# A second form of h2 for the later tiles of an up projection: normalised on the spot, with new homes for f, gates and split tiles

## The chip, the cores and the metric

The kernel runs on one core of one Trainium2 chip, as one program with one launch. The metric is the device time of an execution in microseconds (us). TensorE (PE) multiplies, VectorE (DVE) and ScalarE (ACT) do the elementwise work, GpSimd (POOL) and SyncE (SP) mostly start transfers. Each engine works through its own queue of instructions in order, and waits at an instruction until what it needs is there.

## The reference

One layer of a hybrid backbone over 384 tokens: 128 context tokens and 256 latent tokens, with 2048 channels. Context and latent tokens have modulation vectors of their own (scale, shift and gate, from a conditioning vector). First comes a mixer with three branches and an output projection, then the gated feed-forward part that matters here:

```python
x = x + g1 * rmsnorm(mix, norm_mix_post)
h2 = rmsnorm(x, norm_ffn_pre) * (1 + sc2) + sh2
u, g = jnp.split(h2 @ w_ffn_up, 2, axis=-1)
g = along_cols(lambda t: dwconv(t, ffn_conv_w, ffn_conv_b), g, rows)
f = (jax.nn.gelu(g) * u) @ w_ffn_down
x = x + g2 * rmsnorm(f, norm_ffn_post)
```

`w_ffn_up` is 2048 x 11264, `w_ffn_down` 5632 x 2048, all in float32. The root mean square in `rmsnorm` is over the channels, so its factor is one number per token.

## The kernel before

Activations lie with channels on the 128 partitions and the 384 tokens along the free axis, in 16 tiles of channels, the k tiles. To keep float32 accuracy, both operands of a product are split into a high part (rounded to the matmul's format) and a low part (the rest), and three matmuls are accumulated: high x high, high x low, low x high. Such a group of three is called a triple. ACT writes the high part (L169), DVE the low part (L170).

All weights come through one stream, a list of pieces in the order of use. `run_stream` walks along it. For each piece it issues, in this order: the splits of the pieces up to two ahead (three buffers each for high and low parts, so a split waits until PE has left the piece three before it); if the piece has a `before` function, first the pending `after` functions of the piece ahead of it and then `before`; the matmuls; the pending `after` functions if they are still to be run; and then one step from each of three queues of background work, `bgq[0..2]`, a second one from `bgq[2]` if more than two are left there.

The up projection has 88 tiles of 128 output channels, in turn u and g of the same channels, so that tiles 2n and 2n+1 form pair n. Tiles 0 to 5 are computed together, k tile by k tile (`up0_use`, pieces of 768 columns), while h2 is being made (`h2_step`). Tiles 6 to 87 follow one at a time, each in two pieces of 8 k tiles; piece (t, p) is part p of tile t below. Each tile takes one of four accumulator banks in rotation, and each pair is worked off by three steps on `bgq[2]`: `first` (read the banks), `taps` (the convolution), `last` (Gelu and product), called the after-steps.

The kernel does not wait for the token factor r3 = 1/rms(x) before tile 0. It multiplies the weights with x * S2, where S2 is (1 + sc2) times the norm's weight, and corrects afterwards. The shift is handled by four further columns of the moving operand: H2 for context and latent tokens, as high and low parts (`full`, 388 columns). `first` multiplies the products with r3, and adds the two halves of the shift's products (`hb`), which `taps` and `last` then add as biases. r3 is computed in `close_mx`, which is in the `after` list of the last combined piece: `token_sums` on PE, a Sqrt on ACT, a reciprocal on DVE, a broadcast by PE into a bank, and ACT's copy from there.

Beside the up projection run: the gate g2 (`ada2`, 32 pieces of weights multiplied on DVE with the conditions `MX["cb"]`, which are broadcast by POOL's DMAs and put through a Sigmoid), the transposes of x (`turn_x2`, from tile 12), and `finish_g2`. After it the down projection reads f, 44 k tiles in two halves of the output channels.

Buffers have homes by tag: `hx0` to `hx15` hold the split operand of the projections (448-element pitch, high and low), and pool `F["p"]`, opened in `close_mx`, holds f.

Of the kernel before, what the change touches and what calls it, by code (L numbers as in the profile page):

```python
# [94 lines left out]
def body(ctx: ExitStack, tc: tile.TileContext, i, o):  # L95
# [987 lines left out]
        zt(T_POOL + g, [pool_after(g)])  # L1083


    MX = {}
    mix = [None] * KD
    mx_cm = []

    def open_mx():  # L1090
        flush_bg()
        close_pool(zp_cm[0])
        cm, pool = open_pool("mx", "right")
        mx_cm.append(cm)
        MX["p"] = pool
        conditions(lambda n: pool.tile([P, PIECE], F32, name=name("cb"), tag=f"cb{n}"))

    def conditions(alloc):

        MX["junk"], MX["silu"] = alloc(4), 0  # L1100
        MX["cb"] = [[alloc(2 * c + h) for h in range(2)] for c in range(2)]
        def part(c, h):
            t = MX["cb"][c][h]

            def f():
                act.activation(MX["junk"], t, AF.Sigmoid)
                dve.tensor_mul(t, t, MX["junk"])
                MX["silu"] += 1

            gp.dma_start(t, i["cond2"][c : c + 1, PIECE * h : PIECE * (h + 1)].broadcast_to([P, PIECE]))  # L1110
            bgq[1].append(f)

        for c in range(2):
            for h in range(2):
                part(c, h)

    def gate_after(n, b):
# [50 lines left out]

    def ada2(m, n, half):
        def f(raw):  # L1170
            assert MX["silu"] == 4
            for c in range(2):
                dve.scalar_tensor_tensor(MX["junk"], raw, 1.0, MX["cb"][c][half], ALU.mult, ALU.mult,  # L1173
                                         accum_out=MODR[:, m, n, c, half : half + 1])

        return f
# [175 lines left out]
    fx = [None] * NF  # L1352
    NUP0 = 6

    def up_mm(ps, wh, wl, x, first, last):

        pe.matmul(ps[:, :HW], wh, x.full, start=first, stop=False, skip_group_check=True)  # L1357
        pe.matmul(ps[:, :NT], wh, x.lo, start=False, stop=False, skip_group_check=True)  # L1358
        pe.matmul(ps[:, : NT + 2], wl, x.full[:, : NT + 2], start=False, stop=last, skip_group_check=True)  # L1359
# [10 lines left out]
        return f  # L1370

    def f_tile(n):
        if n % 3 == 0:
            F["t"] = F["p"].tile([P, min(3, NF - n), NT], F32, name=name("f"), tag=f"f{n // 3}")
        return F["t"][:, n % 3]

    def up_after(n):
        st = {}

        def f():  # L1380
            bgq[2].extend((first, taps, last))

        def first():
            pu, pg = acc[("up", 2 * n)], acc[("up", 2 * n + 1)]
            r = R["r3"]
            hb = tmp("hb", 4, bufs=2)
            hb4 = tmp("hb4", 8, bufs=2).rearrange("p (a c) -> p a c", a=2)
            act.activation(hb4[:, 0], pu[:, NT:HW], AF.Copy)
            act.activation(hb4[:, 1], pg[:, NT:HW], AF.Copy)
            dve.tensor_add(hb.rearrange("p (a c) -> p a c", a=2), hb4[:, :, 0:2], hb4[:, :, 2:4])  # L1390
            g = tmp()
            dve.tensor_mul(g, pg[:, :NT], r)
            u = tmp()
            dve.tensor_mul(u, pu[:, :NT], r)
            st.update(hb=hb, g=g, u=u)

        def taps():
            g, hb = st["g"], st["hb"]
            act.activation(g[:, :SEQ], g[:, :SEQ], AF.Identity, bias=hb[:, 2:3])
            act.activation(g[:, SEQ:], g[:, SEQ:], AF.Identity, bias=hb[:, 3:4])  # L1400
            y = tmp()
            w = [v("ffn_conv_w", 3 * n + j) for j in range(3)]
            act.activation(y, g, AF.Identity, bias=v("ffn_conv_b", n), scale=w[1])
            st["y"] = y
            for dst, src, wj in (
                ((1, SEQ), (0, SEQ - 1), w[0]),
                ((0, SEQ - 1), (1, SEQ), w[2]),
                ((SEQ + GRID_W, NT), (SEQ, NT - GRID_W), w[0]),
                ((SEQ, NT - GRID_W), (SEQ + GRID_W, NT), w[2]),
            ):  # L1410
                a = y[:, dst[0] : dst[1]]
                dve.scalar_tensor_tensor(a, g[:, src[0] : src[1]], wj, a, ALU.mult, ALU.add)

        def last():
            y, u, hb = st["y"], st["u"], st["hb"]
            act.activation(y, y, AF.Gelu_apprx_tanh)
            t = f_tile(n)
            dve.scalar_tensor_tensor(t[:, :SEQ], u[:, :SEQ], hb[:, 0:1], y[:, :SEQ], ALU.add, ALU.mult)
            dve.scalar_tensor_tensor(t[:, SEQ:], u[:, SEQ:], hb[:, 1:2], y[:, SEQ:], ALU.add, ALU.mult)
            fx[n] = t  # L1420

        return f
# [5 lines left out]
    def up_use(t, part):  # L1428
        def f(hi, lo):
            if part == 0:  # L1430
                acc["up", t] = accbank()
            for a in range(8):
                k = 8 * part + a
                up_mm(acc["up", t], hi[:, a], lo[:, a], hx[k], k == 0, k == KD - 1)

        return f

    for k in range(KD):
        stream.append(Piece(i["w_up0"][k], (NUP0 * P,), up0_use(k), before=open_f if k == 0 else None,
                            after=[close_mx] + [up_after(n) for n in range(NUP0 // 2)] if k == KD - 1 else None))  # L1440
    a3 = deque()
    for n in range(KD):
        for half in range(2):
            a3.append(Piece(i["w_ada2"][3, n, :, PIECE * half : PIECE * (half + 1)], (PIECE,), None,
                            vec=ada2(3, n, half)))
    for t in range(NUP0, 2 * NF):
        for part in range(2):
            bf = None
            if t == NUP0 + 2 and part == 0:
                bf = lambda: conditions(  # L1450
                    lambda n: F["p"].tile([P, 3 * NT], F32, name=name("cb"), tag=f"f{9 + n}")[:, :PIECE])
            elif t == 2 * NF - 1 and part == 1:
                bf = lambda: down_start()
            elif t == NUP0 + 6 and part == 0:
                bf = lambda: turn_x2()
            elif t == NUP0 + 50 and part == 0:
                bf = lambda: finish_g2()
            stream.append(Piece(i["w_up"][t - NUP0, :, 8 * part : 8 * part + 8], (8, P), up_use(t, part), before=bf,
                                after=[up_after(t // 2)] if t % 2 and part else None))
        if t > NUP0 + 8 and a3:  # L1460
            stream.append(a3.popleft())
    assert not a3

# [27 lines left out]
    def g2_rows():  # L1491

        ps = bgbank()
        pe.transpose(ps[0 : 2 * KD, 0:P], G2.rearrange("p c k -> p (c k)"), ident)
        row = tmp("g2r", P, bufs=1)
        act.activation(row[0 : 2 * KD], ps[0 : 2 * KD, 0:P], AF.Copy)
        gp.dma_start(G2D.rearrange("c (k p) -> (c k) p", p=P), row[0 : 2 * KD])
        g2_load(0)

    def g2_load(h):  # L1500
        t = F["p"].tile([P, 2, HALF_D], F32, name=name("gb"), tag="gb")
        for c in range(2):
            gp.dma_start(t[:, c], G2D[c : c + 1, HALF_D * h : HALF_D * (h + 1)].broadcast_to([P, HALF_D]))
        DN["g", h] = t

    def down_start():
        down_split(0)
# [2 lines left out]
    def down_split(s):  # L1510
        if s >= 2 * NF:
            return
        pr = h_pair(f"hx{s % 3}", NT)
        split(pr.hi, pr.lo, fx[s % NF])
        DN["f", s] = pr

# [7 lines left out]
    def down_use(h, k):  # L1524
        def f(hi, lo):
            if k == 0:
                acc4 = [(rot["acc"] + c) % 4 for c in range(1, 5)]
                free = [4, 5, 6, 7] + acc4[:2] if h == 0 else acc4[2:] + [4, 5, 6, 7]
                DN["ps", h] = [bank(b) for b in free]
            ps = DN["ps", h]  # L1530
            x = DN.pop(("f", h * NF + k))
            down_split(h * NF + k + 2)
            if h == 1 and k >= NF - 3:
                DN["last"] = DN.get("last", []) + [(k, hi, lo, x)]
                if k == NF - 1:
                    down_last(ps)
                return
            for t in range(3):
                for b in range(2):
                    down_mm(ps[2 * t + b], x, hi, lo, t, b, k == 0, k == NF - 1)  # L1540
                if k == NF - 1:
                    for b in range(2):
                        down_out(h, t, b, ps[2 * t + b])
            if k == NF - 1:
                g2_load(1)
                sqrt_table()
# [3 lines left out]
    def down_out(h, t, b, ps):  # L1550

        n = 2 * h + b
        junk = hp.tile([P, NB], F32, name=name("junk"), tag="hx15")
        act.activation(junk, ps, AF.Square, accum_out=ss4[:, t, n : n + 1])
        g = hp.tile([P, NB], F32, name=name("fo"), tag=f"hx{3 + 4 * t + n}")
        dve.tensor_mul(g, ps, DN["g", h][:, min(t, 1), b * NB : (b + 1) * NB])
        fo[t, n] = g

    def down_last(ps):
# [156 lines left out]
```

## Time and profile before

| | |
|---|---|
| median of 3 runs | 2275.97 us (2275.54 to 2276.22) |
| the profiled execution's own time | 2277.23 us |
| its span, first to last instruction | 2275.4 us |
| PE busy | 2237.1 us, 98% |
| DVE busy | 1434.6 us, 63% |
| ACT busy | 881.6 us, 39% |
| mean granted PE clock | 0.993 |

In a row of the timeline stand the start in us from the span's start, the length, the engine, the line, the operation, out<-in, the shapes and the count, and in brackets how long the engine was idle before and what released it. Instructions of one engine overlap at their ends, so the next can start before the one ahead has ended. A row of the stretches view gives, for each engine, busy us and (instructions) in the order PE, weight load, DVE, ACT, POOL, and then the granted clock, the share of DMA and GB/s. A row of a line's own view gives a minimum, median and maximum in ns and the first and last start. The combined tiles 0 to 5 run until about 1208 us, tiles 6 to 87 until about 1906 us, the down projection to the end.

### The profile page before, as it was taken

What the parts mean: (1) busy time and instruction counts of PE and PEld (TensorE: products, weight loads), DVE (VectorE), ACT (ScalarE), POOL (GpSimd) and SP (SyncE); (2) the same over time, 40 slices, a digit from 0 to 9 for tenths busy, and PEclk for the clock granted to TensorE, in tenths of its full rate; (3) what the DMA queues carried; (4) which work ended last, traced back from release to release, by engine and by line L of the source; (5) the groups of instructions that cost most, each with busy time, mean ns of one, the idle gap of its engine ahead of it and who ended that gap; (6) DMA issues with size and microseconds to landing.
All of it is one profiled execution on the core that took longest, in us unless ns stands there. A gap on an engine that the chain in (4) does not pass through costs nothing.

```text
span 2275.4 us, 31790 instructions
## 1 busy us (share of the span) xinstructions
PE 2237.1 (98%) x12553; PEld 2132.7 (94%) x12553; DVE 1434.6 (63%) x2296; ACT 881.6 (39%) x1366; POOL 32.1 (1%) x73
## 2 busy tenths in 40 slices
PE   6999999999999999999989999999999999999998
PEld 3799999999999999999989999999999999888886
DVE  3466777656888888868477577775444445444445
ACT  4443333534223332243376433333333334334333
POOL 0000000000000000000000000000000000000000
PEclk8999999999999999999999999999999999999999
DMA  9944333335766676668433455554433333434343
GB/s 397 392 140 126 123 110 119 121 103 188 232 216 228 224 233 227 222 225 274 139 100 130 138 185 193 180 192 151 140 129 126 124 126 124 130 130 148 130 130 111
DMA packets 104870, 390.06 MB, mean 171 GB/s; under 512 B 12112, under 2 KB 12256, under 8 KB 100624
## 3 DMA queue, kind: packets, MB, share of 16 engines
q1 hardware_dynamic: 100080, 372.81, 48.7%
q0 software_dynamic: 4064, 14.36, 2.0%
q8 instruction: 98, 1.61, 0.3%
q10 hardware_dynamic: 576, 0.86, 0.1%
q14 instruction: 52, 0.43, 0.1%
HBM read 382.71 MB, written 5.27 MB: 171 GB/s over the span
## 4 chain that ended last, share of the span: by engine, by line
PE 96%; DVE 2%; DMA 1%; ACT 1%; issue 1%; DVEq 0%; POOL 0%; SPq 0%; ACTq 0%
PE ps L178 13%; PE ps L180 13%; PE ps L179 13%; PE ps L1357 11%; PE ps L1359 11%; PE ps L1358 11%; PE ps L1521 5%; PE ps L1522 5%; PE ps L1520 5%; PE ps L396 1%; PE ps L898 1%; PE ps L897 1%; PE ps L896 1%; DMA eraw<-w_ada 1%; PE ps L993 1%; PE ps L988 1%
## 5 line engine op out<-in xcount | busy, mean ns | idle before, releaser
L170 DVE TENSOR_TENSOR wlo<-raw,whi 128x1024 fp32r<-128x1024 f32 (+3 forms) x521 | 622.2, 1197 | 706.1 <-ACT whi L169 702.1
L169 ACT ACTIVATE whi<-raw 128x1024 fp32r<-128x1024 f32 (+3 forms) x521 | 539.9, 1039 | 1223.5 <-PE ps L1358 419.7
L178 PE MATMUL ps<-hx,whi 128*128 128x384 f32 x1616 | 546.7, 338 | 2.5 <-ACT whi L169 2.5
L180 PE MATMUL ps<-hx,wlo 128*128 128x384 f32 x1616 | 541.6, 335 | 1.4 <-DVE wlo L170 1.4
L179 PE MATMUL ps<-hx,whi 128*128 128x384 f32 x1616 | 541.4, 335 | 0.2 <-DVE hx L170 0.2
L1357 PE MATMUL ps<-hx,whi 128*128 128x388 f32 x1408 | 481.5, 342 | 4.0 <-DVE hx L1327 4.0
L1359 PE MATMUL ps<-hx,wlo 128*128 128x386 f32 x1408 | 476.6, 339 | 0.0
L1358 PE MATMUL ps<-hx,whi 128*128 128x384 f32 x1408 | 472.4, 336 | 0.0
L1173 DVE SCALAR_TENSOR_TENSOR cb<-raw,cb 128x1024 f32<-128x1024 f32 x256 | 313.2, 1224 | 8.3 <-DMA raw<-w_ada 2.2
L178 PEld LDWEIGHTS ps<-hx,whi 128*128 128x128 f32 x1616 | 304.3, 188 | 9.0 <-ACT whi L169 4.2
L180 PEld LDWEIGHTS ps<-hx,wlo 128*128 128x128 f32 x1616 | 304.2, 188 | 2.6 <-DVE wlo L170 2.6
L179 PEld LDWEIGHTS ps<-hx,whi 128*128 128x128 f32 x1616 | 304.3, 188 | 0.9 <-DVE hx L170 0.5
L1358 PEld LDWEIGHTS ps<-hx,whi 128*128 128x128 f32 x1408 | 270.9, 192 | 0.0
L1357 PEld LDWEIGHTS ps<-hx,whi 128*128 128x128 f32 x1408 | 265.0, 188 | 4.2 <-ACT hx L1313 4.2
L1359 PEld LDWEIGHTS ps<-hx,wlo 128*128 128x128 f32 x1408 | 265.3, 188 | 0.0
L1521 PE MATMUL ps<-whi,hx 128*128 128x512 f32 x528 | 205.5, 389 | 0.8 <-DVE hx L170 0.8
L1520 PE MATMUL ps<-whi,hx 128*128 128x512 f32 x528 | 205.5, 389 | 0.0
L1522 PE MATMUL ps<-wlo,hx 128*128 128x512 f32 x528 | 205.4, 389 | 0.0
L1521 PEld LDWEIGHTS ps<-whi,hx 128*128 128x128 f32 x528 | 99.1, 188 | 21.6 <-DVE hx L170 1.1
L1520 PEld LDWEIGHTS ps<-whi,hx 128*128 128x128 f32 x528 | 99.1, 188 | 21.1 <-ACT hx L169 0.4
L1522 PEld LDWEIGHTS ps<-wlo,hx 128*128 128x128 f32 x528 | 99.1, 188 | 20.4
L703 DVE SCALAR_TENSOR_TENSOR cacc<-cbuf,vec,cacc 128x444 f32<-128x444 f32 x116 | 78.8, 679 | 2.8
(298 smaller groups left out, 1742.8 us busy)
## 6 DMA issues: line engine op xcount, KB each, us to landing
raw<-w_up SPq DMA_DIRECT2D x164, 512.0 KB, 3.7
raw<-w_in SPq DMA_DIRECT2D x163, 512.0 KB, 3.9
raw<-w_ada SPq DMA_DIRECT2D x128, 512.0 KB, 4.3
raw<-w_down SPq DMA_DIRECT2D x88, 512.0 KB, 3.3
eraw<-w_ada SPq DMA_DIRECT2D x32, 1024.0 KB, 16.8
raw<-w_out SPq DMA_DIRECT2D x32, 512.0 KB, 4.6
raw<-w_v SPq DMA_DIRECT2D x16, 512.0 KB, 3.8
raw<-w_br SPq DMA_DIRECT2D x16, 512.0 KB, 4.8
```

The source lines that it names most:

```text
L169: act.activation(hi, src, AF.Copy)
L170: dve.tensor_sub(lo, src, hi.bitcast(F32))
L178: pe.matmul(out, wh, x, start=first, stop=False, skip_group_check=True)
L179: pe.matmul(out, wh, xl, start=False, stop=False, skip_group_check=True)
L180: pe.matmul(out, wl, x, start=False, stop=last, skip_group_check=True)
L1173: dve.scalar_tensor_tensor(MX["junk"], raw, 1.0, MX["cb"][c][half], ALU.mult, ALU.mult, accum_out=MODR[:, m, n, c, half : half + 1])
L1357: pe.matmul(ps[:, :HW], wh, x.full, start=first, stop=False, skip_group_check=True)
L1358: pe.matmul(ps[:, :NT], wh, x.lo, start=False, stop=False, skip_group_check=True)
L1359: pe.matmul(ps[:, : NT + 2], wl, x.full[:, : NT + 2], start=False, stop=last, skip_group_check=True)
L1520: pe.matmul(ps, xh, hi[:, w], start=first, stop=False, skip_group_check=True)
L1521: pe.matmul(ps, xl, hi[:, w], start=False, stop=False, skip_group_check=True)
L1522: pe.matmul(ps, xh, lo[:, w], start=False, stop=last, skip_group_check=True)
```

## The change

From tile 10 on the up projection uses another form of h2, `hy`: x times r3, then scale and shift, split into high and low parts of 384 columns. It is made by `h2_finals`, two k tiles at a time, in the eight pieces of tiles 6 to 9: each of these pieces gets a `before` function, which puts one call of `h2_finals` on `bgq[0]`. Tiles 10 to 87 then use the plain triple `mm3` of three 384-column matmuls. For pairs 5 and up `first` is two copies on ACT, `taps` has no bias passes, and `last` is one multiply on DVE.

`hy` takes the room of f in `F["p"]`, and f for pairs 6 to 37 moves to the `hx` tags. The split tiles of the down projection, its scratch and half of its outputs move to `hy` tags; g2's rows are loaded in four DMAs per half, the first ones from the third piece of the down projection. The conditions for g2 come in two halves (tiles 10 and 34), and its 32 pieces are ordered by half: 16 after tiles 15 to 30, 16 after tiles 38 to 53. `finish_g2` moves from tile 56 to tile 66. The DMA scratch of the program is halved. The core of the diff:

```diff
+    NH2 = 10
+    hy = [None] * KD
+    def y_pair(k, n):
+        t = F["p"].tile([P, 2, HPITCH], F32R, name=name("hy"), tag=f"hy{k}")
...
+    def h2_final(k):
+        st = {}
+        def mul():
+            st["t"] = tmp("hs2", NT, bufs=2)
+            dve.tensor_mul(st["t"], X["x"][:, k], R["r3"])
+        def mod():
+            t = st["t"]
+            act.activation(t[:, :SEQ], t[:, :SEQ], AF.Identity, bias=H2[:, k, 0:1], scale=S2[:, k, 0:1])
+            act.activation(t[:, SEQ:], t[:, SEQ:], AF.Identity, bias=H2[:, k, 1:2], scale=S2[:, k, 1:2])
+            hy[k] = y_pair(k, NT)
+            act.activation(hy[k].hi, t, AF.Copy)
+        def low():
+            dve.tensor_sub(hy[k].lo, st["t"], hy[k].hi.bitcast(F32))
+        return mul, mod, low
+    def h2_finals(k0, k1):
+        parts = [h2_final(k) for k in range(k0, k1)]
+        for n in range(len(parts) + 1):
+            if n < len(parts):
+                parts[n][0]()
+                parts[n][1]()
+            if n:
+                parts[n - 1][2]()
...
     def f_tile(n):
-        if n % 3 == 0:
-            F["t"] = F["p"].tile([P, min(3, NF - n), NT], F32, name=name("f"), tag=f"f{n // 3}")
-        return F["t"][:, n % 3]
+        if n < 6 or n >= 38:
...
+            F["t"] = hp.tile([P, 2, NT], F32, name=name("f"), tag=f"hx{(n - 6) // 2}")
+        return F["t"][:, n % 2]
...
         def first():
             pu, pg = acc[("up", 2 * n)], acc[("up", 2 * n + 1)]
+            if 2 * n >= NH2:
+                g = tmp()
+                act.activation(g, pg[:, :NT], AF.Copy)
+                u = tmp()
+                act.activation(u, pu[:, :NT], AF.Copy)
+                st.update(g=g, u=u)
+                return
...
+                if t < NH2:
+                    up_mm(acc["up", t], hi[:, a], lo[:, a], hx[k], k == 0, k == KD - 1)
+                else:
+                    mm3(acc["up", t][:, :NT], hi[:, a], lo[:, a], hy[k].hi, hy[k].lo, k == 0, k == KD - 1)
...
-            if t == NUP0 + 2 and part == 0:
-                bf = lambda: conditions(
-                    lambda n: F["p"].tile([P, 3 * NT], F32, name=name("cb"), tag=f"f{9 + n}")[:, :PIECE])
+            if t == NH2 and part == 0:
+                bf = lambda: conditions_f(0)
+            elif t == NH2 + 24 and part == 0:
+                bf = lambda: conditions_f(1)
+            elif NUP0 <= t < NH2:
+                bf = lambda q=2 * (t - NUP0) + part: bgq[0].append(lambda: h2_finals(2 * q, 2 * q + 2))
...
-        if t > NUP0 + 8 and a3:
+        if (NH2 + 4 < t and len(a3) > KD or t > NH2 + 27) and a3:
             stream.append(a3.popleft())
...
-        pr = h_pair(f"hx{s % 3}", NT)
+        pr = y_pair(s % 3, NT)
...
-    nc = bacc.Bacc("TRN2", target_bir_lowering=False, num_devices=1, dynamic_dma_scratch_size=4096)
+    nc = bacc.Bacc("TRN2", target_bir_lowering=False, num_devices=1, dynamic_dma_scratch_size=2048)
```

More of the change, by code (lines that the diff above doesn't have):

```diff
@@ L1083, in body @@
         zt(T_POOL + g, [pool_after(g)])
-    MX = {}
+    MX = {"cb": [[None, None], [None, None]]}
     mix = [None] * KD
@@ L1095, in open_mx, with conditions @@
         MX["p"] = pool
+        MX["junk"] = pool.tile([P, PIECE], F32, name=name("cb"), tag="cb4")
         conditions(lambda n: pool.tile([P, PIECE], F32, name=name("cb"), tag=f"cb{n}"))
-    def conditions(alloc):
-        MX["junk"], MX["silu"] = alloc(4), 0
-        MX["cb"] = [[alloc(2 * c + h) for h in range(2)] for c in range(2)]
+    def conditions(alloc, halves=(0, 1)):
+        MX["silu"] = {}
         def part(c, h):
-            t = MX["cb"][c][h]
+            t = alloc(2 * c + h)
+            MX["cb"][c][h] = t
             def f():
@@ L1107, in f @@
                 dve.tensor_mul(t, t, MX["junk"])
-                MX["silu"] += 1
+                MX["silu"][c, h] = True
             gp.dma_start(t, i["cond2"][c : c + 1, PIECE * h : PIECE * (h + 1)].broadcast_to([P, PIECE]))
@@ L1113, in conditions @@
         for c in range(2):
-            for h in range(2):
+            for h in halves:
                 part(c, h)
@@ L1170, in f @@
         def f(raw):
-            assert MX["silu"] == 4
             for c in range(2):
+                assert MX["silu"][c, half]
                 dve.scalar_tensor_tensor(MX["junk"], raw, 1.0, MX["cb"][c][half], ALU.mult, ALU.mult,
@@ L1353, in body @@
     NUP0 = 6
+    NH2 = 10
+    hy = [None] * KD
+    def y_pair(k, n):
+        t = F["p"].tile([P, 2, HPITCH], F32R, name=name("hy"), tag=f"hy{k}")
+        pr = Two()
+        pr.hi, pr.lo = t[:, 0, :n], t[:, 1, :n]
+        return pr
+    def h2_final(k):
[20 more added lines that the diff above has]
+                parts[n - 1][2]()
     def up_mm(ps, wh, wl, x, first, last):
@@ L1372, in f_tile @@
     def f_tile(n):
-        if n % 3 == 0:
-            F["t"] = F["p"].tile([P, min(3, NF - n), NT], F32, name=name("f"), tag=f"f{n // 3}")
-        return F["t"][:, n % 3]
+        if n < 6 or n >= 38:
+            m = n % 3 if n < 6 else (n - 38) % 3
+            if m == 0:
+                F["t"] = F["p"].tile([P, 3, NT], F32, name=name("f"), tag=f"f{n // 3 if n < 6 else 2 + (n - 38) // 3}")
+            return F["t"][:, m]
+        if n % 2 == 0:
+            F["t"] = hp.tile([P, 2, NT], F32, name=name("f"), tag=f"hx{(n - 6) // 2}")
+        return F["t"][:, n % 2]
     def up_after(n):
@@ L1397, in taps @@
         def taps():
-            g, hb = st["g"], st["hb"]
-            act.activation(g[:, :SEQ], g[:, :SEQ], AF.Identity, bias=hb[:, 2:3])
-            act.activation(g[:, SEQ:], g[:, SEQ:], AF.Identity, bias=hb[:, 3:4])
+            g = st["g"]
+            if 2 * n < NH2:
+                hb = st["hb"]
+                act.activation(g[:, :SEQ], g[:, :SEQ], AF.Identity, bias=hb[:, 2:3])
+                act.activation(g[:, SEQ:], g[:, SEQ:], AF.Identity, bias=hb[:, 3:4])
             y = tmp()
@@ L1414, in last @@
         def last():
-            y, u, hb = st["y"], st["u"], st["hb"]
+            y, u = st["y"], st["u"]
             act.activation(y, y, AF.Gelu_apprx_tanh)
             t = f_tile(n)
-            dve.scalar_tensor_tensor(t[:, :SEQ], u[:, :SEQ], hb[:, 0:1], y[:, :SEQ], ALU.add, ALU.mult)
-            dve.scalar_tensor_tensor(t[:, SEQ:], u[:, SEQ:], hb[:, 1:2], y[:, SEQ:], ALU.add, ALU.mult)
+            if 2 * n < NH2:
+                hb = st["hb"]
+                dve.scalar_tensor_tensor(t[:, :SEQ], u[:, :SEQ], hb[:, 0:1], y[:, :SEQ], ALU.add, ALU.mult)
+                dve.scalar_tensor_tensor(t[:, SEQ:], u[:, SEQ:], hb[:, 1:2], y[:, SEQ:], ALU.add, ALU.mult)
+            else:
+                dve.tensor_mul(t, u, y)
             fx[n] = t
@@ L1433, in f, with conditions_f @@
                 k = 8 * part + a
-                up_mm(acc["up", t], hi[:, a], lo[:, a], hx[k], k == 0, k == KD - 1)
-        return f
+                if t < NH2:
+                    up_mm(acc["up", t], hi[:, a], lo[:, a], hx[k], k == 0, k == KD - 1)
+                else:
+                    mm3(acc["up", t][:, :NT], hi[:, a], lo[:, a], hy[k].hi, hy[k].lo, k == 0, k == KD - 1)
+        return f
+    def conditions_f(h):
+        if h == 0:
+            MX["junk"] = F["p"].tile([P, PIECE + 8], F32, name=name("cb"), tag="junk")[:, :PIECE]
+        conditions(lambda n: F["p"].tile([P, 3 * NT], F32, name=name("cb"), tag=f"f{2 + n // 2}")[:, :PIECE], (h,))
     for k in range(KD):
@@ L1441, in body @@
     a3 = deque()
-    for n in range(KD):
-        for half in range(2):
+    for half in range(2):
+        for n in range(KD):
             a3.append(Piece(i["w_ada2"][3, n, :, PIECE * half : PIECE * (half + 1)], (PIECE,), None,
@@ L1448, in body @@
             bf = None
-            if t == NUP0 + 2 and part == 0:
-                bf = lambda: conditions(
-                    lambda n: F["p"].tile([P, 3 * NT], F32, name=name("cb"), tag=f"f{9 + n}")[:, :PIECE])
+            if t == NH2 and part == 0:
[4 more added lines that the diff above has]
+                bf = lambda q=2 * (t - NUP0) + part: bgq[0].append(lambda: h2_finals(2 * q, 2 * q + 2))
             elif t == 2 * NF - 1 and part == 1:
                 bf = lambda: down_start()
-            elif t == NUP0 + 6 and part == 0:
+            elif t == NH2 + 2 and part == 0:
                 bf = lambda: turn_x2()
-            elif t == NUP0 + 50 and part == 0:
+            elif t == NUP0 + 60 and part == 0:
                 bf = lambda: finish_g2()
@@ L1497, in g2_rows @@
         gp.dma_start(G2D.rearrange("c (k p) -> (c k) p", p=P), row[0 : 2 * KD])
-        g2_load(0)
     def g2_load(h):
-        t = F["p"].tile([P, 2, HALF_D], F32, name=name("gb"), tag="gb")
         for c in range(2):
-            gp.dma_start(t[:, c], G2D[c : c + 1, HALF_D * h : HALF_D * (h + 1)].broadcast_to([P, HALF_D]))
-        DN["g", h] = t
+            for b in range(2):
+                t = F["p"].tile([P, NB], F32, name=name("gb"), tag=f"hy{10 + 2 * c + b}")
+                gp.dma_start(t, G2D[c : c + 1, HALF_D * h + NB * b : HALF_D * h + NB * (b + 1)].broadcast_to([P, NB]))
+                DN["g", h, c, b] = t
     def down_start():
@@ L1532, in f @@
             down_split(h * NF + k + 2)
+            if h == 0 and k == 2:
+                g2_load(0)
             if h == 1 and k >= NF - 3:
@@ L1552, in down_out @@
         n = 2 * h + b
-        junk = hp.tile([P, NB], F32, name=name("junk"), tag="hx15")
+        junk = F["p"].tile([P, NB], F32, name=name("junk"), tag="hy3")
         act.activation(junk, ps, AF.Square, accum_out=ss4[:, t, n : n + 1])
-        g = hp.tile([P, NB], F32, name=name("fo"), tag=f"hx{3 + 4 * t + n}")
-        dve.tensor_mul(g, ps, DN["g", h][:, min(t, 1), b * NB : (b + 1) * NB])
+        pool, tag = (F["p"], f"hy{4 + 2 * t + b}") if h == 0 else (hp, f"hx{2 * t + b}")
+        g = pool.tile([P, NB], F32, name=name("fo"), tag=tag)
+        dve.tensor_mul(g, ps, DN["g", h, min(t, 1), b])
         fo[t, n] = g
```

## The prediction

> **What bounds the kernel now.** I read the page first (busy shares, the chain that ended last), then the PE waits from tile 6 of the up projection to the end, then the timelines of PE, ACT and DVE around tile 6, where the change begins.
>
> ```profile
> PE 2237.1 (98%) x12553; PEld 2132.7 (94%) x12553; DVE 1434.6 (63%) x2296; ACT 881.6 (39%) x1366; POOL 32.1 (1%) x73
> PE 96%; DVE 2%; DMA 1%; ACT 1%; issue 1%; DVEq 0%; POOL 0%; SPq 0%; ACTq 0%
> ```
> ```profile
> PE ps L1521 <- DVE hx L170: 0.8, 1, 0.8
> ```
> PE is the bound and the chain is PE's. The second fence is the whole answer of the PE waits from 1216 us to the end (total, times, longest): one wait of 0.8 us, at the start of the down projection. So from tile 6 on time can be won only by PE doing less, and lost as soon as DVE or ACT fall behind.
>
> **What the change takes off PE.** From tile 10 on the matmul triple is 384+384+384 columns in place of 388+384+386. The nearest rows are the triples of today's up tiles and the 384-wide triples of the merge gates, on the same kind of operand pair.
>
> ```profile
> 1854.16 0.34 PE L1357 MATMUL ps<-hx,whi 128*128 128x388 f32 x1
> 1865.75 0.34 PE L1357 MATMUL ps<-hx,whi 128*128 128x388 f32 x1
> ```
> ```profile
> 900.14 0.33 PE L178 MATMUL ps<-hx,whi 128*128 128x384 f32 x1
> 925.10 0.33 PE L178 MATMUL ps<-hx,whi 128*128 128x384 f32 x1
> ```
> Between the first two starts lie 22 triples: 11.59/22 = 0.5268 us. Between the other two lie 48: 24.96/48 = 0.5200 us. Tiles 10 to 87 have 78 x 16 = 1248 triples, so PE does 1248 x 0.0068 = 8.5 us less. The Trainium skill (TensorE: Matmul & The Clock Gate, section Back-to-back issue gap) gives a warm gap of N/2.4 + 2.5 ns; by it six columns are 2.5 ns, and the gain an estimated 3.1 us. The trace shows 6.8 ns for the six, so I take the trace.
>
> **What it costs at the start of tile 6.** Before `before()` of a piece is called, the stream runs the pending `after` work. Today piece (6,0) has no `before`, so `close_mx` (the token scale r3) is issued behind its 24 matmuls. Now it has one, and `close_mx` goes ahead of them. Also, r3 then sits in the bank that tile 6 takes next, so PE must wait for ACT's copy of r3. Around this place the trace of before has (all rows):
>
> ```profile
> 1207.96 1.06 ACT L169 ACTIVATE whi<-raw 128x1024 fp32r<-128x1024 f32 x1 [2.10 <-PE ps L1358]
> 1209.05 1.23 DVE L170 TENSOR_TENSOR wlo<-raw,whi 128x1024 fp32r<-128x1024 f32 x1 [1.93 <-ACT whi L169]
> 1212.15 0.73 PE L310 MATMUL ps<-ones,ss 128*128 128x1 f32 x6
> 1212.91 0.26 ACT L316 ACTIVATE rc<-ps,eps 128x3 f32<-128x3 f32 x1 [3.89 <-PE ps L310]
> 1213.21 0.17 DVE L317 RECIPROCAL rc<-rc 128x3 f32<-128x3 f32 x1 [2.93 <-ACT rc L316]
> 1213.44 0.93 PE L319 MATMUL ps<-ident,rc 128*128 128x128 f32 x6 [0.56 <-DVE rc L317]
> 1214.13 0.42 PE L1357 MATMUL ps<-hx,whi 128*128 128x388 f32 x1
> 1214.41 0.49 ACT L322 ACTIVATE r<-ps 128x384 f32<-128x384 f32 x1 [1.23 <-PE ps L319]
> 1214.85 0.18 ACT L1389 ACTIVATE hb<-ps 128x4 f32<-128x4 f32 x1
> 1215.06 0.17 DVE L1390 TENSOR_TENSOR hb<-hb 128x4 f32<-128x4 f32 x1 [1.68 <-ACT hb L1389]
> 1215.14 0.55 DVE L1392 TENSOR_TENSOR t<-ps,r 128x384 f32<-128x384 f32 x1
> 1215.61 0.55 DVE L1394 TENSOR_TENSOR t<-ps,r 128x384 f32<-128x384 f32 x1
> 1215.73 0.40 ACT L1399 ACTIVATE t<-t,hb 128x128 f32<-128x128 f32 x1 [0.70 <-DVE t L1392]
> 1216.04 0.49 ACT L1400 ACTIVATE t<-t,hb 128x256 f32<-128x256 f32 x1
> 1216.56 0.71 ACT L1403 ACTIVATE t<-t,vec 128x384 f32<-128x384 f32 x1
> 1217.18 1.04 ACT L169 ACTIVATE whi<-raw 128x1024 fp32r<-128x1024 f32 x1
> 1217.30 1.52 DVE L1412 SCALAR_TENSOR_TENSOR t<-t,vec,t 128x127 f32<-128x127 f32 x4 [1.15 <-ACT t L1403]
> 1218.74 1.22 DVE L170 TENSOR_TENSOR wlo<-raw,whi 128x1024 fp32r<-128x1024 f32 x1
> 1218.90 1.28 ACT L1416 ACT_TABLE_LOAD   x1 [0.68 <-DVE t L1412]
> 1220.20 0.53 ACT L1416 ACTIVATE t<-t 128x384 f32<-128x384 f32 x1
> 1220.75 0.35 DVE L1418 SCALAR_TENSOR_TENSOR f<-t,hb,t 128x128 f32<-128x128 f32 x1 [0.80 <-ACT t L1416]
> 1221.42 0.15 DVE L1390 TENSOR_TENSOR hb<-hb 128x4 f32<-128x4 f32 x1
> ```
> Today the block takes PE from 1212.15 to 1214.13, 1.98 us. The split of piece (7,0) starts at 1207.96, the moment PE leaves the last combined piece (it needs that piece's weight buffer); call it time 0. Moved ahead, the sums end at 0.73; the Sqrt and the reciprocal stand behind that split on ACT and DVE. L170 starts at 1.09; DVE issues its next instruction some 0.08 before one ends (L1392 is 0.55 long, L1394 starts 0.47 behind it), so after 1.14. The reciprocal then starts at 2.2, the broadcast at 2.45 (0.23 behind it, as above), the copy at 3.4, and with its 0.49 r3 and PE's tile 6 are free at 3.9 us. Against 1.98 that is 1.9 us more.
>
> **What it costs beside tiles 6 to 9.** The eight pieces of these tiles last 8 x 0.5268 = 4.21 us each. Each gets two k tiles of the new h2: per k tile a multiply and a subtract on DVE, and three passes on ACT. No row shows these, but the same shapes stand above and here:
>
> ```profile
> 1171.70 0.53 ACT L1313 ACTIVATE hx<-sig 128x386 fp32r<-128x386 f32 x1
> 1172.13 0.51 ACT L1320 ACTIVATE t<-x 128x384 f32<-128x384 f32 x1
> 1172.86 0.55 DVE L1326 TENSOR_TENSOR hx<-sig,hx 128x384 fp32r<-128x384 f32 x1
> ```
> DVE alone would need 2 x 0.94 us for the pair (issue 0.47, as L1392 to L1394). But both queues are in order and the work alternates: multiply 0.55; ACT 0.31 + 0.52 (as L1399, L1400, L1403 start), then the copy 0.53, issuing 0.43; the second k tile's passes follow on ACT; its subtract can only start after them. With 0.04 per handover: 0.59 + (0.31+0.52+0.43) + (0.31+0.52+0.53) + 0.04 = 3.25, plus the subtract's 0.47: DVE is held 3.7 us per pair, nearly 1.9 of it waiting. Behind the waiting subtract on DVE stand the after-steps below and then the weight split of the piece two ahead, and PE waits for that split.
>
> Behind each pair come the up projection's own after-steps of pairs 0 to 3, which the stream pops two at a time while more than two are queued. From the rows above: first 1.0 on DVE (0.08 + 2 x 0.47); taps 1.44 on DVE after 1.54 on ACT, of which some 0.6 runs under the last subtract, so 2.4; last 0.7, or 1.4 where it follows taps at once and must wait for the Gelu; the first one 1.3 more for the table. In the order popped: (6,0) first+taps 3.7; (6,1) last+first 2.95; (7,0) taps+last 3.8; (7,1) first 1.3 (0.3 waiting for a split on ACT); (8,0) taps+last 3.8; (8,1) first 1.3; (9,0) taps 2.4; (9,1) last 0.7. Sum 19.95.
>
> DVE's queue up to the split that piece (11,0) waits for: r3 3.9, eight pairs 8 x 3.7 = 29.6, after-steps 19.95, eight splits 8 x 1.14 = 9.1 (the ninth lies ahead of r3). That is 62.55 us. Splits are issued two pieces ahead, so PE would reach (11,0), without waiting, at 10 x 4.21 + 1.98 = 44.1. PE therefore starts it 18.4 us late, the 1.9 of r3 included. The first such wait should be at (8,1). As ends: if DVE never waited within a round, nothing of this would reach PE (rival 1); if the 0.6 under the subtract never overlapped, four taps would add 2.4. I take the value between, since L1412's and L1418's idle times above (1.15 and 0.80 us) show the alternation waiting in full today. It ends there: from pair 5 on the after-steps are shorter (no DVE multiplies, no bias passes, one multiply for two). The two conditions of tile 10 (a Sigmoid with table load, then a multiply) lie beside (10,0) and (10,1) and may add 0.2 at (11,1).
>
> Waits of 3 to 5 us also touch PE's clock. Today's longest wait after the start shows what that does:
>
> ```profile
> 1155.42 0.67 PE L1357 MATMUL ps<-hx,whi 128*128 128x388 f32 x1 [4.00 <-DVE hx L1327]
> 1159.09 0.52 PE L1359 MATMUL ps<-hx,wlo 128*128 128x386 f32 x1
> 1159.41 0.40 PE L1357 MATMUL ps<-hx,whi 128*128 128x388 f32 x1
> ```
> ```profile
> 1154.00:1155.00 1.00, 0.00 (x0) 0.00 (x0) 0.55 (x2) 0.97 (x4) 0.00 (x0) 0.50 0.00 0
> ```
> The granted clock is 0.50, and twelve matmuls from 1155.42 take 3.99 us where 12 x 0.1756 = 2.11 would do: 1.9 us. While DVE is behind, that only shortens the next wait; what can remain is the last one, 0 to 1.9. I take 0.3. The skill (TensorE: Matmul & The Clock Gate, HAM oscillation) names the same thing, idle gaps over about 3.4 us; the trace agrees with its 4.00.
>
> **Edits at nothing.** New homes of f, gates, junk and split pairs: the same instructions in the same order; f6 in hx0 is written after tile 13, its last reader is tile 9. Copies of u and g move from DVE to ACT, and DVE's relief from tile 10 on is worth nothing, as PE waits for neither there. The 32 gate pieces start at tile 15 as before and end at tile 53 instead of 46; the second half's conditions at tile 34 cost two more table loads of 1.28 on ACT, under slack of two pieces (8.4 us). g2's loads become 4 of half the size on POOL, issued in the third down piece and needed 41 pieces later; without that cover they would stop the first down half's end. The halved DMA scratch concerns POOL's queue: at worst its loads would go one after another.
>
> ```profile
> cb<-cond POOLq DMA_DIRECT2D x8, 512.0 KB, 10.5
> ```
> Four conditions in a row would then land after 42 us instead of about 10, and ACT could wait at the merge's start; 0 to some 8 us on PE. No row shows a full ring, so 0.
>
> **Sum.** -8.5 + 18.4 + 0.2 + 0.3 = +10.4 us. The profiled execution took 2277.23, 1.26 above the median of 2275.97; to the median: 2286.4, call it 2286.
>
> **Rivals.** (1) The making of h2 is hidden after all, faster: if the alternation left no idle time on DVE, its issue time would be 8 x 1.14 + 16 x 0.94 + 4 pairs x 3.14 = 36.7 us within 33.7 plus two pieces' slack of 8.4. Then only r3's 1.9 stands against 8.5: 2269.4. It decides once DVE's queue is shorter by 12 us, 1.5 per piece. Against it: DVE already idles 1.15 and 0.80 us for ACT in the same pattern above. (2) Half hidden, stalls of 6 to 13 us: within 0.2% (about 4.6 us, what a measurement of this kernel can tell), some 2277. (3) The smaller gain by the issue gap formula, 8.5 falling to 3.1: 2291.4; the two measured rates speak against it. (4) The ring or the clock costs more: 2288 to 2294.
>
> **Chances.** Forecast (+8 to +13) 0.76, rival 1 0.10, rival 2 0.06, rivals 3 and 4 0.04 each. Slower: 0.76 + 0.08 = 0.84; same 0.06; faster 0.10. The range leaves out rival 1, half of rival 2 and the far end of 4: 2279 to 2291.
>
> **What would show it.** PE waits for DVE's weight splits at (8,1) to (11,0), in sum 15 to 18 us; r3's block before tile 6 of about 3.9 us; DVE nearly without a gap of its own but with waits on ACT; granted clock below 1 there; 0.520 per triple from tile 10 on. It is wrong if the PE waits there stay under 10 us in sum, or the triples keep 0.527.

## The result, and the profile after

| | before | after |
|---|---|---|
| median of 4 runs | 2276.09 us | 2289.51 us (2289.28 to 2290.28) |
| profiled execution, its span | 2277.23, 2275.4 | 2289.28, 2287.5 |

The change makes the kernel slower by 13.4 us; the ratio is 1.006, with a 95% interval of 1.0048 to 1.0071. The prediction said 2286.0 and a range of 2279 to 2291. The +13.4 us is inside that range, but a little above the prediction's own band for the forecast, +8 to +13.

From the page of the changed kernel, the busy shares and the costliest PE group of the new form:

```profile
PE 2236.7 (98%) x12553; PEld 2129.1 (93%) x12553; DVE 1401.3 (61%) x2172; ACT 898.6 (39%) x1336; POOL 34.3 (2%) x77
L178 PE MATMUL ps<-hy,whi 128*128 128x384 f32 x1248 | 418.5, 335 | 1.8 <-ACT whi L169 1.8
```
DVE does 33 us less work than before, and the time still grows. The PE waits of the changed kernel from the r3 block to the end (engine, line and tile that waited, what for; total us, times, longest) stand where before there were two, 0.6 us in the r3 block and 0.8 us at the start of the down projection:

```profile
PE ps L1398 <- ACT whi L169: 6.0, 3, 3.9
PE ps L1400 <- DVE wlo L170: 1.9, 3, 1.0
PE ps L178 <- ACT whi L169: 1.8, 1, 1.8
PE ps L319 <- DVE rc L317: 1.8, 1, 1.8
PE ps L180 <- DVE wlo L170: 1.1, 1, 1.1
PE ps L1591 <- DVE hy L170: 0.8, 1, 0.8
PE ps L1398 <- ACT r L322: 0.6, 1, 0.6
```
Rows 1, 2, 3 and 5 are waits for split weights, 10.8 us, at (8,1), (9,0), (9,1) and (10,1). In 7.8 us of them it is ACT's high part that comes last, and in 3.0 us DVE's low part. Rows 4 and 7 are the r3 block, ahead of tile 6. The combined tiles end at 1207.94 us before and at 1205.71 us after, a difference that has nothing to do with the change. To see the sum free of it, take the stretch from PE's end of the combined tiles 0 to 5 to the first matmul of the down projection. These are the rows of PE's timeline and of the first down matmul's line, before and after:

```profile
L1520 PE MATMUL ps<-whi,hx x528: 389/389/502, 1906.3 to 2266.0; 128*128 128x512 f32 x176
```
```profile
1205.71 0.72 PE L310 MATMUL ps<-ones,ss 128*128 128x1 f32 x6
L1590 PE MATMUL ps<-whi,hy x528: 388/389/501, 1918.3 to 2278.1; 128*128 128x512 f32 x176
```
Before, the sums stood behind piece (6,0), so the stretch begins 8 x 0.5268 = 4.21 us ahead of their 1212.15, and is 1906.3 - 1207.94 = 698.4 us. After, it is 1918.3 - 1205.71 = 712.6 us: +14.2. The down projection and the tail take 369.1 and 369.2 us.

One round of the making of h2, in DVE's timeline of the changed kernel, and what DVE waited for in all of it (idle time before the instructions that touch `hs`, us and times):

```profile
1219.07 1.02 DVE L1372 TENSOR_TENSOR hs<-x,r 128x384 f32<-128x384 f32 x2
1221.23 0.56 DVE L1382 TENSOR_TENSOR hy<-hs,hy 128x384 fp32r<-128x384 f32 x1 [1.15 <-ACT hy L1379]
1222.67 0.56 DVE L1382 TENSOR_TENSOR hy<-hs,hy 128x384 fp32r<-128x384 f32 x1 [0.88 <-ACT hy L1379]
```
```profile
L1376 ACT ACTIVATE hs<-hs,H,S x16: 478/488/496, 1210.6 to 1268.0; 128x128 f32<-128x128 f32 x16
L1377 ACT ACTIVATE hs<-hs,H,S x16: 584/586/589, 1211.0 to 1268.3; 128x256 f32<-128x256 f32 x16
  ACT hy L1379: 16.1, 16
```
A pair holds DVE from 1219.07 to 1222.67 and 0.47 more, 4.07 us, and in the eight pairs DVE idles 16.1 us for ACT's copy. The two scale-and-shift passes take 0.49 and 0.59 us.

ACT waits for DVE as well. The first row below is ACT's idle time before its first pass of each pair, until DVE's multiply; the second is the stretch in which all of h2 is made:

```profile
  DVE hs L1372: 14.8, 8
1210.00:1272.00 62.00, 51.15 (x242) 47.99 (x242) 38.60 (x76) 41.62 (x82) 0.00 (x0) 0.87 0.19 64
```
DVE is busy for 38.6 and ACT for 41.6 of these 62 us, so neither is full: each stands waiting for the other in turn.

### The profile page after: what moved, and what is told of

It is laid out like the page before. It is cut to its first block, busy times and chain, and to the rows that moved or that the text cites. A ratio compares the mean times of both kernels' runs of the same rounds, so it can differ in the third digit from the quotient of the medians.

```text
span 2287.5 us, 31664 instructions
## 1 busy us (share of the span) xinstructions
PE 2236.7 (98%) x12553; PEld 2129.1 (93%) x12553; DVE 1401.3 (61%) x2172; ACT 898.6 (39%) x1336; POOL 34.3 (2%) x77
## 4 chain that ended last, share of the span: by engine, by line
PE 94%; DVE 2%; ACT 2%; DMA 1%; issue 1%; DVEq 0%; SPq 0%; ACTq 0%
PE ps L178 23%; PE ps L180 23%; PE ps L179 23%; PE ps L1591 5%; PE ps L1590 5%; PE ps L1592 5%; PE ps L396 1%; PE ps L898 1%; PE ps L897 1%; PE ps L896 1%; PE ps L1398 1%; PE ps L1399 1%; PE ps L1400 1%; DVE wlo L170 1%; DMA eraw<-w_ada 1%; PE ps L993 1%
## 5 line engine op out<-in xcount | busy, mean ns | idle before, releaser
L178 PE MATMUL ps<-hx,whi 128*128 128x384 f32 x1616 | 547.2, 339 | 1.5 <-ACT whi L169 1.5
L179 PE MATMUL ps<-hx,whi 128*128 128x384 f32 x1616 | 541.9, 335 | 0.2 <-DVE hx L170 0.2
L178 PE MATMUL ps<-hy,whi 128*128 128x384 f32 x1248 | 418.5, 335 | 1.8 <-ACT whi L169 1.8
L180 PE MATMUL ps<-hy,wlo 128*128 128x384 f32 x1248 | 418.5, 335 | 1.3 <-DVE wlo L170 1.1
L179 PE MATMUL ps<-hy,whi 128*128 128x384 f32 x1248 | 417.9, 335 | 0.0
L178 PEld LDWEIGHTS ps<-hx,whi 128*128 128x128 f32 x1616 | 304.3, 188 | 7.9 <-ACT whi L169 6.6
L180 PEld LDWEIGHTS ps<-hx,wlo 128*128 128x128 f32 x1616 | 304.2, 188 | 2.4 <-DVE wlo L170 2.4
L179 PEld LDWEIGHTS ps<-hx,whi 128*128 128x128 f32 x1616 | 304.4, 188 | 0.9 <-DVE hx L170 0.5
L180 PEld LDWEIGHTS ps<-hy,wlo 128*128 128x128 f32 x1248 | 234.7, 188 | 2.4 <-DVE wlo L170 2.4
L178 PEld LDWEIGHTS ps<-hy,whi 128*128 128x128 f32 x1248 | 234.9, 188 | 2.2 <-ACT whi L169 2.1
L179 PEld LDWEIGHTS ps<-hy,whi 128*128 128x128 f32 x1248 | 234.9, 188 | 0.0
L1591 PE MATMUL ps<-whi,hy 128*128 128x512 f32 x528 | 205.7, 390 | 0.8 <-DVE hy L170 0.8
L1590 PE MATMUL ps<-whi,hy 128*128 128x512 f32 x528 | 205.7, 390 | 0.0
L1592 PE MATMUL ps<-wlo,hy 128*128 128x512 f32 x528 | 205.6, 389 | 0.0
L1591 PEld LDWEIGHTS ps<-whi,hy 128*128 128x128 f32 x528 | 99.1, 188 | 21.5 <-DVE hy L170 1.1
L1590 PEld LDWEIGHTS ps<-whi,hy 128*128 128x128 f32 x528 | 99.1, 188 | 21.0 <-ACT hy L169 0.4
```

The lines of the kernel that those rows point to most:

```text
L178: pe.matmul(out, wh, x, start=first, stop=False, skip_group_check=True)
L179: pe.matmul(out, wh, xl, start=False, stop=False, skip_group_check=True)
L180: pe.matmul(out, wl, x, start=False, stop=last, skip_group_check=True)
L1590: pe.matmul(ps, xh, hi[:, w], start=first, stop=False, skip_group_check=True)
L1591: pe.matmul(ps, xl, hi[:, w], start=False, stop=False, skip_group_check=True)
L1592: pe.matmul(ps, xh, lo[:, w], start=False, stop=last, skip_group_check=True)
```

## The experiments

The theory after the result: DVE's in-order queue, held by its alternation with ACT, sets when PE reaches tile 11; the triples give back 8.5 us. Two of the runs, e2_gain and e3_nomod, leave out parts of the computation, as said with each.

**e1_late: the r3 block behind piece (6,0) again.**

```diff
-            elif NUP0 <= t < NH2:
-                bf = lambda q=2 * (t - NUP0) + part: bgq[0].append(lambda: h2_finals(2 * q, 2 * q + 2))
...  in up_use, behind the matmuls
+            if t < NH2:
+                q = 2 * (t - NUP0) + part
+                bgq[0].append(lambda: h2_finals(2 * q, 2 * q + 2))
```


> The changed kernel with the r3 block issued behind the matmuls of piece (6,0) again; the making of h2 is unchanged. Theory: the queue of DVE, held by its alternation with ACT, sets when PE reaches tile 11, and it starts with r3. r3 is then ready at 7.0 us after the last combined piece instead of 4.0, so all of it moves 3 us: about 2292.5 us, 3 above the changed kernel, with the PE waits before tile 11 at some 18 us. Rival (the block ahead of tile 6 costs PE its own 1.9 us, as the sum of the prediction counts it): 1.9 less, 2287.6 us.

Measured: 2293.3 us (ratio to before 1.0075, interval 1.006 to 1.009), 3.8 above the changed kernel; the stretch is 715.2 us, +2.6, and the rest lies outside it. Its PE waits for splits come to 13.6 us:

```profile
PE ps L1398 <- ACT whi L169: 7.3, 3, 3.9
PE ps L1400 <- DVE wlo L170: 3.1, 5, 1.2
PE ps L180 <- DVE wlo L170: 1.8, 2, 1.1
PE ps L178 <- ACT whi L169: 1.4, 1, 1.4
```
So within the changed kernel the block's new place is a gain: PE loses time at tile 6, but DVE's first multiply comes 4.3 instead of 7.0 us behind the combined tiles, 2.7 us sooner, and PE waits for what stands in DVE's queue. The rival is out. The waits themselves are fewer than the 18 us named; the rest of the loss is matmuls that follow each other more slowly behind the waits, as shown below for the changed kernel.

**e2_gain: the narrow triple alone.** From tile 10 on the kernel before uses

```diff
+                    mm3(acc["up", t][:, :NT], hi[:, a], lo[:, a], hx[k].full[:, :NT], hx[k].lo, k == 0, k == KD - 1)
```
and the shorter after-steps; no `hy` is made, and the token factor and the shift are left out there.

> The kernel before, with the 384-column triple and the shorter after-steps from tile 10 on, but on the old unscaled h2 and with nothing new made beside tiles 6 to 9 (the token factor and the shift are left out for pairs 5 and up). Theory: only the gain is left, 1248 triples at 0.5200 instead of 0.5268 us, 8.5 us: 2267.5 us, and no PE wait from tile 6 on but the one of 0.8 us. Rival (the issue gap formula, an estimate of 3.1 us for the six columns): 2273 us.

Measured: 2268.25 us (0.9963, interval 0.995 to 0.9976); the stretch is 690.1 us, 8.3 less than before. This agrees with the 8.5 of the two measured rates, and not with the rival's 3.1. The rival's formula stands in the Trainium skill (TensorE: Matmul & The Clock Gate, Back-to-back issue gap) as the gap of an isolated matmul; that section itself does not give it for a stream of weight loads and matmuls.

**e3_nomod: the alternation shortened.** In `h2_final` the two Identity passes on ACT are dropped; DVE's instructions stay.

> The changed kernel without the two scale and shift passes on ACT in each k tile of the new h2 (scale and shift are left out from tile 10 on); the multiplies, the copies and the subtracts stay. Theory: DVE's hold per pair falls from 4.1 to about 2.1 us, its waiting for ACT with it; the PE waits before tile 11 shrink from 13 to about 4 us, and the kernel comes to about 2273.5 us, some 16 below the changed one. Rival (DVE's busy time is the bound): DVE does the same work, so the time stays within 2 us of 2289.5.

Measured: 2275.94 us (1.0, interval 0.9991 to 1.001), 13.6 below the changed kernel. The PE waits for splits come to 2.5 us, where about 4 were expected. In DVE's timeline a pair is now two multiplies and two subtracts without a gap:

```profile
1226.85 1.01 DVE L1372 TENSOR_TENSOR hs<-x,r 128x384 f32<-128x384 f32 x2
1227.98 1.03 DVE L1380 TENSOR_TENSOR hy<-hs,hy 128x384 fp32r<-128x384 f32 x2
```
That is 2.1 us for the pair in place of 4.07, with the same DVE work, so waiting for ACT, and not DVE's busy time, made the loss. This run also takes 16 us of work off ACT; that ACT's own busy time was the limit is ruled out by the 14.8 us that ACT idled for DVE in the changed kernel, and not by this run. It missed the expected 2273.5 by 2.4 us. The start of it is in PE's timeline and in the granted clock (the column behind the five engines) after the r3 block, the rest in the timelines of ACT and DVE:

```profile
1211.68 0.69 PE L1396 MATMUL ps<-hx,whi 128*128 128x388 f32 x1 [0.58 <-ACT r L322]
1212.17 0.53 PE L1397 MATMUL ps<-hx,whi 128*128 128x384 f32 x1
1216.67 0.43 PE L1396 MATMUL ps<-hx,whi 128*128 128x388 f32 x1
1212.00:1214.00 2.00, 2.00 (x7) 2.00 (x7) 1.88 (x6) 1.12 (x4) 0.00 (x0) 0.50 0.21 82
1218.36 1.06 ACT L169 ACTIVATE whi<-raw 128x1024 fp32r<-128x1024 f32 x1 [2.40 <-PE ps L1397]
1219.45 1.22 DVE L170 TENSOR_TENSOR wlo<-raw,whi 128x1024 fp32r<-128x1024 f32 x1 [1.94 <-ACT whi L169]
```
Fifteen matmuls from 1211.68 to 1216.67 take 4.99 us where 15 x 0.1756 = 2.63 would do. Behind the block the clock is at half, and this costs 2.4 us that neither the prediction nor this expectation counted. A slower PE alone would only shorten its later waits. But PE also leaves piece (6,0) late, and the split of (7,1) needs that piece's buffer: ACT waits 2.40 us for PE and DVE 1.94 us for ACT, and so DVE's queue itself falls back by 1.9 us. The remaining 0.5 us were not looked into. In the changed kernel DVE does not stand idle at this split, as it is still busy with the after-steps.

**e4_spread: one pair in every second piece, from (8,1) to (15,1).** With `NH2` at 16, what hangs on it moves six tiles too: the triples and shorter after-steps, the conditions, the gate pieces and the transposes.

```diff
-    NH2 = 10
+    NH2 = 16
...  in up_use, behind the matmuls, in place of the `before` of tiles 6 to 9
+            if 8 <= t < NH2 and part:
+                q = t - 8
+                bgq[0].append(lambda: h2_finals(2 * q, 2 * q + 2))
```


> The changed kernel with the new h2 made in every second piece from (8,1) to (15,1), one pair each, used from tile 16 on, and r3 behind piece (6,0)'s matmuls. Theory: with one pair per two pieces DVE has 8.4 us for two splits (2.3), one pair (4.1) and 1.5 after-steps, and does not fall behind; PE waits for no split, and the gain is 72 x 16 x 0.0068 = 7.8 us: 2268.2 us, faster than both kernels. Rival (making h2 costs PE time wherever it is made, as contention or clock): it stays above 2276.

Measured: 2268.16 us (0.9965, interval 0.9951 to 0.9979), faster than both kernels; the stretch is 690.7 us, -7.6. From the r3 block to the end of the up projection PE has one wait, that of the block itself, as before the change. DVE's idle time beside `hs` up to 1290 us, 14 of the 16 k tiles:

```profile
PE ps L319 <- DVE rc L317: 0.6, 1, 0.6
```
```profile
  ACT hy L1379: 14.1, 14
```
DVE idles as long per k tile as in the changed kernel (1.0 us). The waiting has not gone; it lies where DVE has room. The rival is out.

**e5_spread_early: e4 with the r3 block ahead of piece (6,0).** Piece (6,0) gets a `before` that does nothing.

> The version with the new h2 spread over pieces (8,1) to (15,1), with the r3 block ahead of piece (6,0)'s matmuls, as in the changed kernel. Here DVE is not behind, so PE pays for the block in full. Theory now: the block's place costs 2.0 us of waiting, and the idle stretch also halves the granted clock for the first 15 or so matmuls of tile 6, as the traces of the changed kernel and of the one without scale passes show (15 matmuls in 5.0 us instead of 2.6), 2.4 us: 4.4 above the spread version, about 2272.5 us. Rival (the prediction's price, waiting alone, 1.9 us): 2270 us. Rival (the block costs nothing, since DVE gets r3 earlier): 2268.

Measured: 2272.75 us (0.9988, interval 0.9978 to 0.9997), 4.6 above e4_spread; the stretch is 695.6 us, +4.9. Its PE waits are the block's alone, and the clock falls behind them:

```profile
PE ps L319 <- DVE rc L317: 1.8, 1, 1.8
PE ps L1398 <- ACT r L322: 0.6, 1, 0.6
```
```profile
1210.22 1.35 PE L319 MATMUL ps<-ident,rc 128*128 128x128 f32 x6 [1.75 <-DVE rc L317]
1212.00:1214.00 2.00, 1.85 (x6) 1.85 (x7) 1.10 (x3) 1.27 (x6) 0.00 (x0) 0.50 0.44 158
```
Where DVE is not behind, the block's place costs 4.6 to 4.9 us, more than twice the prediction's 1.9. Both rivals are out.

**e7_soon: e4 begun two tiles earlier, beside the pending pairs.** `NH2 = 14`, pairs in (6,1), (7,1) to (13,1).

> The spread version begun earlier: pairs of k tiles in every second piece from (6,1) to (13,1), beside the after-steps of pairs 0 to 3, used from tile 14 on; r3 behind piece (6,0). Theory: same density, but the three pairs of after-steps that are pending from tiles 0 to 5 lie beside it, so DVE falls behind by some 7.5 us up to tile 14 (PE waits of 1 to 2 us each at (8,0), (9,0), (10,0) and (12,0)); the gain is 74 x 16 x 0.0068 = 8.1 us: 2275.5 us. Rival (only the density counts, one pair in two pieces is hidden): 2268 us.

Measured: 2275.06 us (0.9998, interval 0.9989 to 1.0008), 6.9 above e4_spread at the same density. Its PE waits up to the end of the up projection:

```profile
PE ps L1400 <- DVE wlo L170: 3.4, 4, 1.1
PE ps L1398 <- DVE t L1447: 1.1, 1, 1.1
PE ps L1398 <- ACT whi L169: 0.4, 1, 0.4
```
They lie at the four pieces that were named, (8,0), (9,0), (10,0) and (12,0); the 1.1 us of the second row are a wait for a bank that `first` still reads on DVE. So density alone doesn't decide; the after-steps of the three pairs that tiles 0 to 5 leave at once fill DVE's room in tiles 6 to 9.

## Why the prediction was right, point by point

- *The gain of 8.5 us.* Right: 8.3 in e2_gain, 7.6 of an expected 7.8 in e4_spread (72 tiles).
- *The r3 block, +1.9 us.* The mechanism was right: PE stands there from 1205.71 to tile 6's first matmul at 1210.04, 4.3 us for the 3.9 of the prediction. The price was too low where PE is the bound: with the half clock behind it, 4.6 to 4.9 us (e5_spread_early). In the changed kernel the missing part doesn't show, since PE waits for DVE's queue afterwards anyway, and that it doesn't was luck: the prediction did not ask what the block does to the clock. e1_late shows that the early block even helps there.
- *DVE's queue, PE 18.4 us late at (11,0).* Right in kind, and shown by e3_nomod and e4_spread, though most of the waiting ended with ACT's high part, whose splits stand behind passes that wait for DVE, and not with DVE's low part. The term that was mis-sized is the 3.7 us of a pair: 4.07 measured, 3.0 us over eight pairs. I had taken the ACT passes from rows with a bias or a scale alone (0.40 and 0.49); with both from columns they take 0.49 and 0.59, four times 0.09 in the chain of a pair. The Trainium skill (ScalarE: Activation LUTs, What ACT_TABLE_LOAD costs) says that each such column operand adds about 93 ns; the trace agrees, with 0.09 and 0.10 us. The stretch lost 14.2 + 8.5 = 22.7 us against the 18.9 of the sum, 3.8 more. DVE's queue up to the split of (11,0) accounts for it. These are the split of (7,0), which is the prediction's time 0, the first multiply, the last split, and the matmul of (11,0) that needs it:

```profile
1205.73 1.06 ACT L169 ACTIVATE whi<-raw 128x1024 fp32r<-128x1024 f32 x1 [2.10 <-PE ps L1399]
1210.02 1.03 DVE L1372 TENSOR_TENSOR hs<-x,r 128x384 f32<-128x384 f32 x2 [1.88 <-ACT r L322]
1270.88 1.23 DVE L170 TENSOR_TENSOR wlo<-raw,whi 128x1024 fp32r<-128x1024 f32 x1
1272.15 0.45 PE L180 MATMUL ps<-hy,wlo 128*128 128x384 f32 x1
```
  The queue is free at 1270.88 + 1.14, 66.3 us behind time 0, where the prediction had 62.55. Of these 3.7 us the pairs make 3.0; the first multiply starts 4.3 us behind time 0 instead of 3.9; and the after-steps, which are what is left, come to 20.3 instead of 19.95.
- *Waits of 15 to 18 us.* Too many: 10.8 us, and just above the 10 us that the prediction had named as a sign of being wrong. Of the 22.7 us, 2.35 are the r3 block (4.33 for 1.98), and some 9.5 are matmuls that follow each other more slowly, 7.5 of them in (6,0), (9,1) and (10,1). There the clock was at half: in (6,0) behind the block, as in e5_spread_early, and after the longest wait and after those of (10,1), as these stretches of the changed kernel show:

```profile
1251.00:1255.00 4.00, 3.75 (x11) 3.24 (x12) 2.69 (x4) 2.27 (x5) 0.00 (x0) 0.50 0.37 125
1267.00:1270.00 3.00, 3.00 (x11) 3.00 (x11) 1.05 (x3) 2.94 (x8) 0.00 (x0) 0.50 0.50 171
```
  The prediction had said that a slower PE only shortens the next wait while DVE is behind, and took 0.3 us for what remains. The trace agrees: at (11,0) the third matmul starts at 1272.15, 0.04 us behind the end of the split that it needs. The forecast of the waits had not taken the slower matmuls off.
- *Edits at nothing.* The new homes, g2's loads, the later gate pieces and the halved scratch are all in e4_spread too, which gains within 0.2 us of the triples' due. Together they cost nothing that can be measured; the scratch was not tried alone.
- *Rivals.* Rival 1 (hidden) fell by the waits, but e4_spread shows that it needed only another place; rival 3 (smaller gain) fell by e2_gain. By its time the result also fits rival 4 (the ring or the clock costs more, 2288 to 2294). It is out for another reason: DVE's queue, and not the clock, sets when PE passes (11,0), and the halved scratch costs nothing in e4_spread.

## What to carry to other kernels

In these runs, work put beside a busy PE cost what it held an in-order queue for, waits on the other engine included, and not its busy time: 1.9 us of DVE work held DVE for 4.1. Place such work where the queue has room (not next to a backlog), at a density at which the weight splits still come two pieces ahead. A callback that changes the order of issue by one piece is part of a change too.

## What the runs showed of the hardware that was not expected

The granted clock fell to 0.50 behind the r3 block although no single idle time in it was over 1.8 us, less than half of the 4.00 us from which the prediction had read the half clock: some 4.4 us with only a few small matmuls were enough (e5_spread_early, from 1207.74 to 1212.15). In the changed kernel the same happened at (10,1), behind waits of 1.8 and 1.1 us with two matmuls between them, while behind those of 1.7 and 0.6 us at (8,1) the clock stayed at 1.00, as this stretch shows:

```profile
1234.00:1240.00 6.00, 3.87 (x20) 3.55 (x21) 3.47 (x6) 4.17 (x8) 0.00 (x0) 1.00 0.27 89
```
What decides between the two no run here shows. And the six columns fewer per triple, which had given 6.8 ns in the rows before, gave 8.3 us in e2_gain, or 6.7 ns for each of the 1248 triples; why six columns are worth so much no run shows.
